# 28 of 76 projection groups by seven half-size products, with the weight scale worked out on GpSimd

## The chip, the cores and the metric

The kernel runs on one core of one Trainium2 chip. The metric is the device time of one execution in microseconds, the median over runs. The engines go by the names of the profile: PE is TensorE (matmul), PEld its weight loads, DVE is VectorE, ACT is ScalarE, POOL is GpSimd, and SP is SyncE, which issues most transfers. PSUM is the memory that TensorE writes to, SBUF the memory on the core that all engines read, and DRAM holds inputs, outputs and spilled data.

## The reference

Two layers run one after the other over 512 tokens of width 2048. Each layer projects the normalised input once, feeds three groups of heads, and projects their joined outputs back into the residual.

```
h    = x * rsqrt(mean(x*x) + EPS) * norm_g                # 512 x 2048
proj = h @ w_in                                           # 2048 x 8208, split by columns:
       # conv h,b,c,gate: 512 each; attention q,k,v,gate: 1024 each;
       # linear attention q,k: 256 each, v,gate: 512 each, low rank: 16
y_conv = cv_b * (conv3(cv_c * cv_h) + bias) * silu(cv_g)
q, k   = rmsnorm(sb_q), rmsnorm(sb_k)                     # 8 heads of 128
y_sb   = stick_breaking(q, k, v) * silu(sb_g)             # causal, 128 queries at a time
   # z = q.k; log_keep = log_sigmoid(-z); w = exp(log_sigmoid(z) + sum of later log_keep); out = w @ v
g      = log_sigmoid(gl_lr @ w_up + b_up) / 16
y_gla  = rmsnorm(gla(q, k, v, g)) * silu(gl_g)            # 4 heads, chunks of 64 with a state
x      = x + concat(y_conv, y_sb, y_gla) @ w_out          # 2048 x 2048
```

Everything is float32. Nearly all of the multiplications are in `h @ w_in` and `mix @ w_out`.

## The kernel before, in words

**Groups.** The columns of `w_in` (2048 x 8208) and `w_out` (2048 x 2048) are cut into groups of 256, one of them with the 16 low-rank columns on top. `specs` lists them in the order of their use: per layer 6 for the linear attention, 4 for the first half of the convolution, 16 for the attention (four times value, gate, query, key), 4 for the second half of the convolution, and 8 for the output, so 38 per layer and 76 in all.

**Two float16 parts.** TensorE multiplies float16. Every float32 operand is scaled by a power of two and split into a high part (rounded) and a low part (what the rounding left). A product is high x high + low x high + high x low, three matmuls for every one of the reference.

**A group's way.** `fetch` (called two groups ahead, transfers by SP) brings two halves of 1 MB, 128 partitions x 8 x 256, into `stage`. `wmax` (L319) squares each half on ScalarE and keeps the sums. `wscale` (from L329) adds them over partitions on GpSimd (`wgm`) and makes from the sum, on VectorE, the scale `ws` and its inverse `wu` in five or six instructions on single numbers (L330 to L348). `whi` (L392) writes the high parts on ScalarE, `wlo` (L399) the low parts on VectorE. `load` does all of it for group i+1 when group i is taken up, at high priority; the squares of a group are kept behind the last high part of the group before.

**Products.** `project_cols` (L568 to L570) keeps a block of weights stationary and moves all 512 tokens: 96 matmuls of 512 columns. `project_toks` (L576 to L578) keeps activations of 128 tokens stationary and moves the 256 columns of the group: 192 matmuls. `project_by_token` (L601) is the same, token block by token block. Results go to two PSUM banks of `psp`, which has three.

**The activations** are in `xh` and `xl`, and for the output in `mh` and `ml` (`mix`). Each of the 16 blocks of the joined branch outputs is split as soon as it is made, in `mixsplit`, each branch with a scale of its own (`mixscale`, column j of `pmix`); the weights of the output groups take the ratio of these scales into account block by block (`weight_ratio`, `wsr`).

**Attention.** `attend` puts four pieces of work into the list `later` (`scores` of two heads, `values` of two heads); `go` runs one of them between the projections of the next step. The gate of a branch (`gate`) is silu by exponent and logarithm.

**Output.** For each output group the old residual comes from DRAM into `qT`; `finish` (L1078) adds `psp` times `wu` to it on VectorE, stores the sum, and in the first layer squares it (L1084, ScalarE) for the next layer's norm.

**Order.** Each engine executes its instructions in the order in which the program was scheduled; a waiting instruction holds up those behind it on its engine. The start is written out by hand; elsewhere the order follows from the code, the priorities and the number of buffers in each pool (`stage` 3 halves, `wpool` 3 pairs of parts, `psp` 3 banks).

Of the kernel before, what the change touches and what calls it, by code (L numbers as in the profile page):

```python
# [20 lines left out]
XBITS = 8.0  # L21
RED = bass_isa.ReduceOp

# [7 lines left out]
CHUNKS = ((((3, 0), (2, 512)), (3, 2)), (((0, 0), (1, 128)), (0, 1)))  # L31


@with_exitstack
def hybrid_trunk(ctx, tc, x, norm_g, w_in, conv_w, conv_b, sb_qn_g, sb_kn_g,
# [10 lines left out]
    GX = GW + LR  # L46
    NG = D // GW
# [4 lines left out]
    big = ctx.enter_context(tc.tile_pool(name="big", bufs=4))  # L52
# [32 lines left out]
    xs = dram.tile([seq, D], F32, tag="xs", name="xs")  # L85
    xt = [newbig("x", [P, 2, D], F32) for _ in range(2)]
# [22 lines left out]
    parno = wk([P, 32], "raw", 1)  # L109
# [130 lines left out]

    V.tensor_scalar(xsc.bitcast(I32), xun.bitcast(I32), -1.0, float(254 << 23), ALU.mult, ALU.add)
# [30 lines left out]
    specs = []  # L272
    for l in range(depth):
        for cols in ([(GL_V, GW)], [(GL_V + GW, GW), (GL_LR, LR)], [(GL_Q, GW)], [(GL_K, GW)],
                     [(GL_G, GW)], [(GL_G + GW, GW)]):
            specs.append((l, w_in, cols))
        conv = [[(l, w_in, [(c0 + j * GW, GW)]) for c0 in (CV_H, CV_C, CV_G, CV_B)] for j in range(2)]
        specs += conv[0]
        for j in range(4):
            for c0 in (SB_V, SB_G, SB_Q, SB_K):  # L280
                specs.append((l, w_in, [(c0 + j * GW, GW)]))
        specs += conv[1]
        for gi in range(NG):
            specs.append((l, w_out, [(gi * GW, GW)]))
# [10 lines left out]
    def junk(n):  # L295

        return wk([P, HK * GX], "junk", 1, dt=U8)[:, :n]


    def fetch(i):  # L300

        l, src, cols = specs[i]
        staged[i] = st = []
        for h in range(2):
            s_ = stage.tile([P, HK, GX], F32, tag="st", name=nm("st"))
            o = 0
            for c0, w in cols:
                nc.sync.dma_start(
                    s_[:, :, o:o + w],
                    src[l, h * HK * P:(h + 1) * HK * P, c0:c0 + w].rearrange("(k p) n -> p k n", p=P))  # L310
                o += w
            st.append(s_)

    def wmax(i, h):

        n = sum(c[1] for c in specs[i][2])
        if h == 0:
            peak[i] = sm(2, "wm")
        S.activation(junk(HK * n).rearrange("p (k n) -> p k n", k=HK), staged[i][h][:, :, :n], AF.Square,  # L319
                     accum_out=peak[i][:, h:h + 1])  # L320

    def wscale(i):

        l, src, cols = specs[i]

        m = sm(1, "wq")
        if i:
            gm = sm(2, "wgm")
            G.partition_all_reduce(gm, peak.pop(i), P, RED.add)  # L329
            V.tensor_scalar(m, gm[:, 0:1], gm[:, 1:2], 2.0 ** -120, ALU.add, ALU.max)  # L330
        else:
# [5 lines left out]
            V.tensor_scalar(m, ps, 2.0 ** -120, None, ALU.max)  # L337
        V.tensor_scalar(m.bitcast(I32), m.bitcast(I32), 0x7F000000, None, ALU.bitwise_and)
        sc = sm(1, "ws")
        V.tensor_scalar(sc.bitcast(I32), m.bitcast(I32), -0.5, float(204 << 23), ALU.mult, ALU.add)  # L340
        p2 = sm(1, "wp")
        V.tensor_scalar(p2.bitcast(I32), m.bitcast(I32), 0.5, float(50 << 23), ALU.mult, ALU.add)
        u = sm(1, "wu", bufs=6)
        sw = None
        if src is w_out:
            sw = sm(8, "wsr")
            V.tensor_scalar(sw, ratio[l][0], sc, None, ALU.mult)
# [781 lines left out]
```

## Time and profile before

| What | Value | How to read it |
|---|---|---|
| time of the runs | 1742.44 us, median of 3 (1742.14 to 1742.74) | the metric |
| span of the profiled execution | 1740.9 us | first to last instruction of one execution |
| TensorE (PE) | 1726.8 us busy, 12,846 matmuls | idle 7.7 us of the first 40, 2.0 between 890 and 1020, 3.7 after 1560 |
| VectorE (DVE) | 1068.9 us busy, 2015 instructions | 282.3 us of it low parts of the `w_in` groups |
| ScalarE (ACT) | 1090.0 us busy, 1460 instructions | 285.5 us squares, 317.9 us high parts of weights |
| GpSimd (POOL) | 75.1 us busy, 104 instructions | 47.0 us of it sums over partitions for the weight scales |
| transfers | 204.69 MB, 118 GB/s on average | 1 MB halves of weights land 5.3 to 5.5 us after issue |

A row of the grouped view reads: line, engine, operation, output and inputs by the names in the program, their shapes, the count; then busy time in all, mean duration of one in ns; then the idle time of the engine just ahead of them and what ended it. A row of the timeline begins with start and duration. The first layer's output groups run up to about 890 us of the span, the second layer's from about 1560 us to the end.

### The profile page before, as it was taken

The numbers are of one execution on the slowest core, as the hardware profiler recorded it, in microseconds if no ns is written. First come the engines' busy times: TensorE is split into PE (matmuls) and PEld (weight loads), VectorE is DVE, ScalarE is ACT, GpSimd is POOL, SyncE is SP. The second block draws the span as 40 slices with busy tenths as digits, with TensorE's granted clock in tenths as the row PEclk, the third lists the DMA queues.
The fourth block names the chain that finished last, engine by engine and source line by source line (L and its number), as shares of the span: only waits on it lengthen the run. The fifth ranks groups of instructions, "written<-read, shape, count | busy, mean of one in ns | idle before, by whom it ended". The sixth has DMA issues, their size and how long they took to land.

```text
span 1740.9 us, 30651 instructions
## 1 busy us (share of the span) xinstructions
PE 1726.8 (99%) x12846; PEld 1232.4 (71%) x12846; DVE 1068.9 (61%) x2015; ACT 1090.0 (63%) x1460; POOL 75.1 (4%) x104
## 2 busy tenths in 40 slices
PE   8999999999999999999999999999999999999999
PEld 6744556868787754788885455668686868448888
DVE  7556788657665747433474576976575666673431
ACT  7558577667575867455555684766767667663540
POOL 1000000000000000000010000000000000000000
PEclk9999999999999999999999999999999999999999
DMA  6333313335353545444463333133454444453531
GB/s 222 121 97 97 98 58 113 103 104 131 108 140 110 128 121 128 134 158 146 138 148 105 97 97 97 50 121 110 125 124 109 117 124 126 112 132 113 177 124 40
DMA packets 266121, 204.69 MB, mean 118 GB/s; under 512 B 93106, under 2 KB 265212, under 8 KB 265472
## 3 DMA queue, kind: packets, MB, share of 16 engines
q1 hardware_dynamic: 256976, 193.29, 39.0%
q10 hardware_dynamic: 9008, 9.45, 1.6%
q8 instruction: 100, 1.64, 0.4%
q14 instruction: 37, 0.30, 0.1%
HBM read 173.36 MB, written 8.39 MB: 104 GB/s over the span
## 4 chain that ended last, share of the span: by engine, by line
PE 48%; issue 7%; DVE 1%; DMA 1%; SPq 0%; POOL 0%; ACT 0%; POOLq 0%; DVEq 0%
PE psp L576 8%; PE psp L578 8%; PE psp L577 8%; PE psp L570 6%; PE psp L568 6%; PE psp L569 6%; PE psp L601 3%; PE psz L749 1%; PE psm L988 1%; PE psz L944 1%; PE psz L840 0%; DMA m<-raw 0%; DVE wl L399 0%; SPq L487 0%; DMA xs<-x 0%
## 5 line engine op out<-in xcount | busy, mean ns | idle before, releaser
L577 PE MATMUL psp<-wl,m 128*128 128x256 f16 x1664 | 454.0, 273 | 0.0
L578 PE MATMUL psp<-wh,m 128*128 128x256 f16 x1664 | 453.9, 273 | 0.0
L576 PE MATMUL psp<-wh,m 128*128 128x256 f16 x1664 | 453.8, 273 | 0.0
L399 DVE SCALAR_TENSOR_TENSOR wl<-st,ws,wh 128x2048 f16<-128x2048 f32 (+1 forms) x120 | 282.3, 2353 | 193.1 <-ACT wh L392 179.7
L392 ACT ACTIVATE wh<-st,ws 128x2048 f16<-128x2048 f32 (+1 forms) x118 | 236.3, 2003 | 202.6 <-PE psp L569 100.9
L319 ACT ACTIVATE junk<-st 128x2048 uint8<-128x2048 f32 (+1 forms) x150 | 285.5, 1903 | 7.6 <-DMA st<-in_w_out_dram 4.5
L577 PE MATMUL psp<-wl,x 128*128 128x256 f16 x768 | 209.5, 273 | 0.0
L578 PE MATMUL psp<-wh,x 128*128 128x256 f16 x768 | 209.5, 273 | 0.0
L576 PE MATMUL psp<-wh,x 128*128 128x256 f16 x768 | 209.4, 273 | 0.0
L570 PE MATMUL psp<-m,wl 128*128 128x512 f16 x512 | 194.4, 380 | 0.0
L568 PE MATMUL psp<-x,wh 128*128 128x512 f16 x512 | 194.4, 380 | 0.0
L569 PE MATMUL psp<-x,wh 128*128 128x512 f16 x512 | 194.4, 380 | 0.0
L569 PE MATMUL psp<-m,wh 128*128 128x512 f16 x512 | 194.4, 380 | 0.0
L568 PE MATMUL psp<-m,wh 128*128 128x512 f16 x512 | 194.4, 380 | 0.0
L570 PE MATMUL psp<-x,wl 128*128 128x512 f16 x512 | 194.3, 380 | 0.0
L570 PEld LDWEIGHTS <-wl 128*128 128x128 f16 x1024 | 100.1, 98 | 122.8 <-issue 3.7
L569 PEld LDWEIGHTS <-wh 128*128 128x128 f16 x1024 | 100.1, 98 | 117.5 <-issue 1.1
L568 PEld LDWEIGHTS <-wh 128*128 128x128 f16 x1024 | 100.1, 98 | 115.3 <-issue 0.5
L576 PEld LDWEIGHTS <-m 128*128 128x128 f16 x1664 | 162.7, 98 | 19.9 <-issue 0.7
L578 PEld LDWEIGHTS <-m 128*128 128x128 f16 x1664 | 162.6, 98 | 19.4 <-issue 0.5
L577 PEld LDWEIGHTS <-m 128*128 128x128 f16 x1664 | 162.6, 98 | 18.8
L392 ACT ACTIVATE wh<-st,wsr 128x512 f16<-128x512 f32 x128 | 81.6, 710 | 100.5 <-PE psp L578 74.4
(285 smaller groups left out, 2260.4 us busy)
## 6 DMA issues: line engine op xcount, KB each, us to landing
st<-in_w_in_dram SPq DMA_DIRECT2D x120, 1024.0 KB, 5.3
st<-in_w_out_dram SPq DMA_DIRECT2D x32, 1024.0 KB, 5.5
x<-in_x_dram SPq DMA_DIRECT2D x4, 1024.0 KB
qT<-in_x_dram ACTq DMA_DIRECT2D x8, 512.0 KB, 5.3
qT<-xs ACTq DMA_DIRECT2D x8, 512.0 KB
xs<-x SPq DMA_DIRECT2D x14, 256.0 KB, 4.5
out_dram<-kT SPq DMA_DIRECT2D x14, 256.0 KB, 3.7
th<-za SPq DMA_TRANSPOSE x64, 3.6
```

The source lines that it names most:

```text
L319: S.activation(junk(HK * n).rearrange("p (k n) -> p k n", k=HK), staged[i][h][:, :, :n], AF.Square, accum_out=peak[i][:, h:h + 1])
L392: lasthi[i] = S.activation(wh[:, ks, :n], staged[i][h][:, ks, :n], AF.Copy, scale=s_)
L399: V.scalar_tensor_tensor(wl[:, ks, :n], staged[i][h][:, ks, :n], s_, wh[:, ks, :n], ALU.mult, ALU.subtract)
L568: T.matmul(o, wh[:, kk, cs], xh[:, :, k, :], start=st_, stop=False)
L569: T.matmul(o, wh[:, kk, cs], xl[:, :, k, :], start=False, stop=False)
L570: T.matmul(o, wl[:, kk, cs], xh[:, :, k, :], start=False, stop=en)
L576: T.matmul(o, ah[:, t, k, :], wh[:, kk, :n], start=st_, stop=False, skip_group_check=True)
L577: T.matmul(o, ah[:, t, k, :], wl[:, kk, :n], start=False, stop=False, skip_group_check=True)
L578: T.matmul(o, al[:, t, k, :], wh[:, kk, :n], start=False, stop=en, skip_group_check=True)
L601: T.matmul(o[:, :n], a_[:, t, k, :], w[k // HK][part][:, k % HK, :n], start=i == 0 and k == 0, stop=i == 2 and k == KT - 1)
L749: T.matmul(o, src16[sb][a][:, ss], tgt16[tb][b][:, g0:g1].rearrange("p g h c -> p (g h c)"), start=i == 0, stop=i == 2)
L944: T.matmul(z[:, o:o + (t + 1) * P], qT[:, a_, t, hh, :], kT[:, b_, :t + 1, hh, :], start=i == 0 and o % 512 == 0, stop=False, skip_group_c ...
```

## The change

**Seven products.** A group that the table `SEVEN` marks is computed as a 2 x 2 block product: the tokens in two halves of 256, the input width in two halves of 1024, and the columns in two halves of 128. Instead of eight block products there are seven, of sums and differences of blocks. Marked are, per layer, the gate and key groups of the four attention steps, the first group of the second half of the convolution, and output groups 2 to 6: 14 per layer, 28 in all. `cols7` has the weights stationary (gate and convolution groups), `toks7` the activations (key and output groups).

**Weights.** For a marked group `right` makes seven quarter parts (128 x 1024), with four sums or differences of the staged quarters on VectorE between them; `wpool` holds six quarter tiles with high and low part, `stage` four halves.

**Activations.** The sums of blocks are made once a layer for the input (`x_sums`, placed behind the low-rank gate: four operations on each of two tiles, eight splits, and transposing transfers by SP) and once a layer for the mix (`mix_sums`).

**Evictions.** `seven` leaves the results in four quarters, made from pieces in PSUM: `Raw` puts them together without scale, `Residual` with scale and the old residual.

**The scale.** `wscale` does its arithmetic on GpSimd behind the sum over partitions, in four instructions (`wq` twice, `ws`, `wu`); group 0 stays on VectorE. The power of two is taken by rounding the exponent with a large constant. Output groups use one scale for the whole mix, so the ratio is gone.

**The mix.** Branch outputs are spilled to DRAM unsplit (`spill` into `mixd`), loaded back into two tiles `m32` during the second half of the convolution (`mix_load`), and split there with the one scale of `mix_unit`.

**Values one step later.** The `values` of a step's second head are held until the next step, between its two `scores`.

**Shorter chains.** `gate` has three ScalarE operations on half a gate instead of five, `scores` two VectorE operations fewer on each chunk, and the sum over partitions of the value bound (`bgm`) is gone. Small products of scales (`nu`, `vu`, `qu2`, `uu`) are made on GpSimd.

```diff
-XBITS = 8.0
+XBITS = 7.0
+MAGIC = 12582912.0
+SEVEN = {"gla": (), "conv0": (), "sb": (1, 3), "conv1": (0,), "out": (2, 3, 4, 5, 6)}
...
-    stage = ctx.enter_context(tc.tile_pool(name="stage", bufs=3))
-    wpool = ctx.enter_context(tc.tile_pool(name="wpool", bufs=3))
+    stage = ctx.enter_context(tc.tile_pool(name="stage", bufs=4))
+    wpool = ctx.enter_context(tc.tile_pool(name="wpool", bufs=6))
...
     def wscale(i):
...
             G.partition_all_reduce(gm, pk, P, RED.add)
+            if pk.shape[-1] > 2:
+                G.tensor_tensor(gm[:, 0:1], gm[:, 0:1], gm[:, 2:3], ALU.add)
+            E = G
+            E.tensor_scalar(m, gm[:, 0:1], gm[:, 1:2], 2.0 ** -120, ALU.add, ALU.max)
...
+        E.tensor_scalar(m, m.bitcast(I32), 2.0 ** -24, MAGIC, ALU.mult, ALU.add)
         sc = sm(1, "ws")
+        E.tensor_scalar(sc.bitcast(I32), m, -(2.0 ** 23), (MAGIC + 204) * 2.0 ** 23, ALU.mult, ALU.add)
         u = sm(1, "wu", bufs=6)
+        E.tensor_scalar(u.bitcast(I32), m, 2.0 ** 23, ratio[l] if src is w_out else xub[:, l:l + 1],
+                        ALU.mult, ALU.add)
...
+    def right(i):
+        a, b = (staged[i][0][:, :, c * P:(c + 1) * P] for c in range(2))
+        c, d = (staged[i][1][:, :, c * P:(c + 1) * P] for c in range(2))
+        def part(x):
+            w = wtile(i)
+            hi, lo = (w[:, h, :HK * P].rearrange("p (k n) -> p k n", n=P) for h in range(2))
+            his.setdefault(i, []).append(S.activation(hi, x, AF.Copy, scale=scales[i]))
+            V.scalar_tensor_tensor(lo, x, scales[i], hi, ALU.mult, ALU.subtract)
+        part(a)
+        V.tensor_tensor(b, b, d, ALU.add)
+        V.tensor_tensor(a, a, b, ALU.add)
+        part(a)
+        part(c)
+        V.tensor_tensor(c, c, a, ALU.add)
+        V.tensor_tensor(a, a, d, ALU.subtract)
+        part(a)
+        part(b)
+        part(d)
+        part(c)
     def load_(i):
-        with tc.issue_after(lasthi[i - 1].ins):
+        with tc.issue_after(his[i - 1][min(1, len(his[i - 1]) - 1)].ins):
...
+    def seven(left, by_cols, evict):
...
+        o1 = bank(psp, "p")
+        product(o1, 0, True, False)
+        with tc.high_priority():
+            s1 = tmp("s1")
+            S.activation(s1, o1[:, :2 * P], AF.Copy, scale=ev.unit)
+        o2 = bank(psp, "p")
+        product(o2, 1, True, True)
+        with tc.high_priority():
+            u2 = tmp("u2")
+            ev.add(u2, o2[:, :2 * P], s1)
+        product(o1, 2, False, True)
+        ev.first(o1[:, :2 * P])
+        o3 = bank(psp, "p")
+        product(o3, 3, True, True)
...
+            ev.sub(vv, o3[:, :2 * P], u2)
+        o4 = bank(psp, "p")
+        product(o4, 4, True, False)
+        ev.last4(vv, o4[:, :2 * P])
+        product(o2, 5, True, True)
+        ev.plus(0, 1, o2[:, :2 * P], vv)
+        product(o4, 6, False, True)
+        ev.plus(1, 0, o4[:, :2 * P], u2)
...
+    def column_sums(pieces):
+        tt = V.tensor_tensor
+        for x11, x12, x21, x22 in pieces:
+            tt(x22, x21, x22, ALU.subtract)
+            tt(x21, x11, x21, ALU.subtract)
+            tt(x11, x22, x11, ALU.subtract)
+            tt(x12, x12, x11, ALU.add)
...
+        def mix_sums(s_):
...
+            for i, (th, kh) in ((1, (0, 0)), (0, (1, 1)), (2, (1, 0)), (3, (0, 1))):
...
+                for k in (0, HK // 2):
...
+                    S.activation(a, y, AF.Copy, scale=s_)
+                    V.scalar_tensor_tensor(b, y, s_, a, ALU.mult, ALU.subtract)
...
+            prior = held.pop() if held else lambda: None
+            if j < 3:
+                held.append(lambda: values(1))
+                later.extend((lambda: scores(0), prior, lambda: scores(1), lambda: values(0)))
...
+        y = conv_in(1, go)
+        m32 = mix_load()
+        s_ = conv_out(1, y, go)
...
+        for k in (0, 4, 6, 8, 12, 14, 10, 2):
+            mix_split(k, s_)
+        if any(modes[cursor[0]:cursor[0] + NG]):
+            sums = mix_sums(s_)
...
+            def last4(self, vv, ps):
...
+                V.tensor_tensor(r, self.like(vv), r, ALU.add)
+                with tc.high_priority():
+                    V.scalar_tensor_tensor(dst, self.like(ps), self.nu, r, ALU.mult, ALU.add)
```

**What moves.** In the rows below names carry buffer numbers; a row gives line, operation, output and inputs, and the shape.

GpSimd in the attention steps of the first layer, before: `wgm` is the sum over partitions of a group's squares, `bgm` that of the bound of the values.

```order
L169 ISA bgm_623_5169<-bm_578_4742 128x1
L329 ISA wgm_640_5240<-wm_636_5234 128x2
L329 ISA wgm_669_5516<-wm_665_5510 128x2
L329 ISA wgm_699_5800<-wm_695_5794 128x2
L329 ISA wgm_724_6082<-wm_720_6076 128x2
```

The same engine and stage with the change, where `wq`, `ws` and `wu` are the steps of the scale:

```order
L348 ISA
L348 ISA wgm_786_7166<-wm_782_7160 128x2
L352 ISA
L352 TENSOR_SCALAR wq_785_7165<-wgm_786_7166 128x1
L361 TENSOR_SCALAR wq_785_7165<-wq_785_7165 128x1
L363 TENSOR_SCALAR ws_787_7170<-wq_785_7165 128x1
L365 TENSOR_SCALAR wu_788_7172<-wq_785_7165,xub_155 128x1
L1257 TENSOR_SCALAR qu2_843_7871<-wu_788_7172 128x1
L348 ISA
L348 ISA wgm_823_7481<-wm_819_7475 128x2
```

Each sum over partitions now has an unnamed instruction ahead of it and another behind it, and four steps of arithmetic follow on the same engine.

ScalarE in the first layer's output groups, before: `junk, wm` are the squares of the next group's halves, `wh` its high parts, and L1084 the squares of the residual.

```order
L319 ACTIVATE junk_998_8571,wm_997_8570<-st_973_8316 128x2048
L319 ACTIVATE junk_999_8573,wm_997_8570<-st_974_8318 128x2048
L392 ACTIVATE wh_1006_8588<-st_973_8316,wsr_1005_8585 128x2x256 x4
L392 ACTIVATE wh_1008_8598<-st_974_8318,wsr_1005_8585 128x2x256 x4
L1084 ACTIVATE junk_1012_8804,ssq_903_7559<-x_901_7557 128x256
```

The same engine in the first marked output group with the change. `s1` is its first piece out of PSUM; the parts with scale `ws_992` are its own, those with `ws_1015` the next group's.

```order
L335 ACTIVATE junk_1011_9291,wm_1010_9290<-st_985_9033 128x2048
L680 ACTIVATE s1_1025_9378<-psp_1024_9329,wu_993_9049 128x256
L429 ACTIVATE w_997_9064<-st_964_8792,ws_992_9047 128x1024
L429 ACTIVATE w_998_9067<-st_964_8792,ws_992_9047 128x1024
L429 ACTIVATE w_999_9070<-st_965_8794,ws_992_9047 128x1024
L429 ACTIVATE w_1000_9073<-st_965_8794,ws_992_9047 128x1024
L335 ACTIVATE junk_1012_9293,wm_1010_9290<-st_986_9035 128x2048
L429 ACTIVATE w_1017_9304<-st_985_9033,ws_1015_9300 128x1024
L429 ACTIVATE w_1018_9309<-st_985_9033,ws_1015_9300 128x1024
L429 ACTIVATE w_1019_9312<-st_986_9035,ws_1015_9300 128x1024
```

The second square of the next group now stands behind the last part of this one, and the next group's first part directly behind that square.

VectorE at the same place with the change. `vv` and `x` are pieces of the output of the group with `wu_993`, `qT` its old residual.

```order
L1343 SCALAR_TENSOR_TENSOR vv_1029_9529<-psp_1028_9480,wu_993_9049,u2_1027_9429 128x256
L1354 TENSOR_TENSOR qT_1007_9284<-vv_1029_9529,qT_1007_9284 128x2x128
L1360 TENSOR_TENSOR qT_1007_9284<-vv_1029_9529,qT_1007_9284 128x2x128
L1356 SCALAR_TENSOR_TENSOR x_958_8783<-psp_1030_9531,nu_1031_9580,qT_1007_9284 128x2x128
L430 SCALAR_TENSOR_TENSOR w_1017_9304<-st_985_9033,ws_1015_9300,w_1017_9304 128x1024
L434 TENSOR_TENSOR st_985_9033<-st_985_9033 128x8x128
L1362 SCALAR_TENSOR_TENSOR x_957_8782<-psp_1026_9380,wu_993_9049,qT_1007_9284 128x2x128
L430 SCALAR_TENSOR_TENSOR w_1018_9309<-st_985_9033,ws_1015_9300,w_1018_9309 128x1024
L430 SCALAR_TENSOR_TENSOR w_1019_9312<-st_986_9035,ws_1015_9300,w_1019_9312 128x1024
L1362 SCALAR_TENSOR_TENSOR x_958_8783<-psp_1030_9531,wu_993_9049,qT_1007_9284 128x2x128
```

Before, both low parts of the next group stood ahead of a group's two output pieces; now the next group's first low part stands between the second and the third of four pieces, with one of its sums behind it, and two more low parts ahead of the last piece.

More of the change, by code (lines that the diff above doesn't have):

```diff
@@ L407, in load_ @@
         wscale(i)
-        for h in range(2):
-            whi(i, h)
-            wlo(i, h)
+        if modes[i]:
+            right(i)
+            return
+        for q in range(4):
+            whi(i, q)
+            wlo(i, q)
     def weights():
@@ L519, in hybrid_trunk @@
     xlow(0, 1, mix, True)
-    wlo(0, 0)
-    wlo(0, 1)
+    for q in range(4):
+        wlo(0, q)
     xhigh(1, 0, mix)
@@ new lines, in project_by_token, with quarters, own @@
+    def project_by_token(n):
+        w, u = weights()
+        for t in range(NT):
+            o = bank(psp, "p")
+            for i, (a_, part) in enumerate(((xh, 0), (xl, 0), (xh, 1))):
+                for k in range(KT):
+                    T.matmul(o[:, :n], a_[:, k, t, :], wview(w, part, k, n),
+                             start=i == 0 and k == 0, stop=i == 2 and k == KT - 1)
+            yield t, o, u
+    def quarters(sums):
+        def own(th, kh):
+            return [a[:, kh * HK:(kh + 1) * HK, 2 * th:2 * th + 2, :] for a in mix]
+        return own(0, 0), sums[1], own(0, 1), sums[0], sums[2], sums[3], own(1, 1)
```

575 lines of the change are left out of this document (357 added, 218 removed).

## The prediction

> **What bounds the kernel now.** I read the head of the page first, then who waited for whom on TensorE, then its timeline, then the stretches by stage, and last the groups by form on the engines that feed it.
>
> ```profile
> span 1740.9 us, 30651 instructions
> ...
> PE 1726.8 (99%) x12846; PEld 1232.4 (71%) x12846; DVE 1068.9 (61%) x2015; ACT 1090.0 (63%) x1460; POOL 75.1 (4%) x104
> ...
> PEclk9999999999999999999999999999999999999999
> ...
> PE 48%; issue 7%; DVE 1%; DMA 1%; SPq 0%; POOL 0%; ACT 0%; POOLq 0%; DVEq 0%
> ```
>
> TensorE is busy in 99% of the span at full granted clock, and the chain that ended last is its own work. A busy TensorE could still be a slow one, so its pace is read from the timeline, with start and duration in front.
>
> ```profile
> 30.26 1.91 PE L601 MATMUL psp<-wh,x 128*128 128x256 f16 x16
> 32.01 1.91 PE L601 MATMUL psp<-wl,x 128*128 128x256 f16 x16
> ...
> 157.98 1.50 PE L749 MATMUL psz<-m 128*128 128x128 f16 x24
> 159.32 0.38 PE L568 MATMUL psp<-x,wh 128*128 128x512 f16 x1
> 159.54 0.38 PE L569 MATMUL psp<-x,wh 128*128 128x512 f16 x1
> 159.75 0.38 PE L570 MATMUL psp<-x,wl 128*128 128x512 f16 x1
> ...
> 1716.33 20.97 PE psp L601 x192
> ```
>
> From start to start: 512 columns take 0.216 us, 256 columns 1.75/16 = 0.109, 128 columns 1.34/24 = 0.0558. A group of 192 matmuls of 256 columns takes 20.97 us, one of 96 matmuls of 512 takes 96 x 0.216 = 20.7. The engine runs at the pace of its columns, so fewer columns are time, if weights and activations keep coming.
>
> **The change part by part.** *Products.* 18 of the 28 groups have the activations stationary: 192 matmuls of 256 become 336 of 128, 336 x 0.0558 = 18.75 us, 2.22 less each, 40.0 in all. Ten have the weights stationary: 96 of 512 become 168 of 256, 168 x 0.109 = 18.4, 2.33 less each, 23.3 in all. Together -63.3 us. No matmul is added elsewhere; attention and the linear-attention part keep theirs. With the profiled execution's 1740.9 and the 1.5 us by which the median 1742.4 of the runs stands above it, the floor is 1679.
>
> *What feeds the products.*
>
> ```profile
> L399 DVE SCALAR_TENSOR_TENSOR wl<-st,ws,wh 128x2048 f16<-128x2048 f32 x116 | 272.4, 2349 | 186.7 <-ACT wh L392 173.2 <-PE psz L946 10.2 <-PE psz L749 2.9
> L1054 DVE SCALAR_TENSOR_TENSOR qp<-raw,qp 128x1024 f16<-128x1024 f32 x16 | 19.6, 1226 | 18.0 <-ACT qp L1053 18.0
> L902 DVE TENSOR_TENSOR kT<-kT,g 128x1024 f32<-128x1024 f32 x4 | 4.9, 1222 | 0.1
> L1078 DVE SCALAR_TENSOR_TENSOR kT<-psp,wu,qT 128x256 f32<-128x256 f32 x4 | 1.9, 484 | 18.8 <-PE psp L601 18.8
> L770 DVE TENSOR_TENSOR e<-raw 128x256 f32<-128x256 f32 x24 | 10.1, 422 | 3.1 <-PE psm L679 2.8
> L1053 ACT ACTIVATE qp<-raw 128x1024 f16<-128x1024 f32 x16 | 16.9, 1057 | 44.0 <-DVE raw L1049 25.8 <-DVE raw L1044 18.1
> L319 ACT ACTIVATE junk<-st 128x2048 uint8<-128x2048 f32 x146 | 277.4, 1900 | 7.5 <-DMA st<-in_w_out_dram 4.5 <-DMA st<-in_w_in_dram 1.2
> L319 ACT ACTIVATION_READ_ACCUMULATOR junk<-st 128x1 f32 x150 | 28.0, 187 | 0.0
> L1084 ACT ACTIVATE junk<-x 128x256 uint8<-128x256 f32 x32 | 13.3, 416 | 65.8 <-DVE x L1078 65.0 <-ACT junk L1084 0.3
> ```
>
> A plain group costs VectorE two low parts, 2 x 2.35 = 4.7 us. A seven-product group costs seven low parts of 1024 elements (7 x 1.23 = 8.6) and four adds (4 x 1.22 = 4.9), 13.5. Its output pieces, where they go into the residual, are six PSUM operations of 256 (6 x 0.48) and three adds (3 x 0.42), 4.2. That is 17.7 us for 18.75 us of TensorE: 94%.
>
> ```profile
> 340.00:640.00 300.00, 300.00 (x2401) 231.16 (x2399) 191.18 (x328) 205.99 (x247) 14.67 (x17) 1.00 0.47 121
> 705.00:890.00 185.00, 184.19 (x1665) 162.38 (x1663) 82.45 (x164) 99.02 (x172) 3.38 (x9) 1.00 0.51 151
> ```
>
> The columns are length, then busy time of PE, PEld, DVE, ACT, POOL, then clock and DMA. In the attention stage (first row) DVE is 64% and ACT 69% busy; eight of sixteen groups there get 8.8 more on DVE, less what the shorter score chain, gate and scale arithmetic give back. It stays under 80%. In the output stage (second row) DVE was 45% busy and goes beyond 90%, since the mix's splitting and sums (8 adds and 16 low parts of 1024, 29 us a layer) come on top. That cover is nearly gone; I allow 0.3 us for each of the 28 groups, 8 us, for output pieces that come late: each now has one product, 2.7 us, before TensorE wants the bank. The DRAM round trip costs nothing as long as its load hides behind the last three plain convolution groups, 62 us.
>
> *The scale on GpSimd.* Here a wait is added on the path that makes the weights.
>
> ```profile
> 740.52 0.19 ACT L319 ACTIVATION_READ_ACCUMULATOR junk<-st 128x1 f32 x1
> 742.26 2.56 ACT L392 ACTIVATE wh<-st,wsr 128x512 f16<-128x512 f32 x4 [1.55 <-DVE wu L348]
> ...
> 412.60 3.06 POOL L329 PARTITION_ALL_REDUCE wgm<-wm  x1 [21.40 <-ACT junk L319]
> ...
> 411.59 2.35 DVE L399 SCALAR_TENSOR_TENSOR wl<-st,ws,wh 128x2048 f16<-128x2048 f32 x1
> 413.85 1.56 DVE L965 TENSOR_TENSOR zw<-zw,za 128x895 f32<-128x895 f32 x2
> ...
> L169 POOLq MODIFY_POOL_CONFIG  x2: 11/11/11, 30.3 to 30.3; - x2
> ...
> 30.40 0.73 POOL L169 PARTITION_ALL_REDUCE kgm<-kg  x2
> ```
>
> From the last square to the first high part took 1.55 us. Two things lengthen that. First, an all-reduce of 0.4 us takes 3.06 where VectorE runs operations with two SBUF inputs back to back, and ends just behind them; GpSimd's steps (0.2 each, between VectorE's 0.15 and more) will meet that often. I take 2.0 us for reduce, three steps and such waits (1.0 to 4). Second, the order shows an unnamed GpSimd instruction ahead of every all-reduce and another ahead of the arithmetic; the kernel before has one, ahead of its first all-reduce, and there the trace has MODIFY_POOL_CONFIG. The change has 156. The one ahead of an all-reduce runs while it waits for the squares; the one behind it does not. Call its price t. The low end is the row: 0.1 us until the reduce starts. But the kernel before asks for one kind of code only, so no exchange need have taken place. If code has to come from DRAM, the nearest rows are landings:
>
> ```profile
> st<-in_w_in_dram SPq DMA_DIRECT2D x120, 1024.0 KB, 5.3
> ...
> st<-in_w_in_dram SPq DMA_DIRECT2D x4, 64.0 KB, 15.3
> ...
> ngr<-in_norm_g_dram ACTq DMA_DIRECT2D x1, 16.0 KB, 1.9
> ```
>
> 1.9 to 15.3 us; I take t = 5.3, the common landing, since an exchange is likelier than none. [...]
>
> Where t is hidden: in the attention stage long and short gaps between squares and first high part alternate on ACT (13 and 2 us of other work); ACT has some 30% idle there, eight short gaps of 5 us fit. Where it is not: in the first layer's output groups 2 to 6, where the first high part stands directly behind the squares. ACT's round there is seven high parts 7.4, two squares with their reads 4.2, four residual squares 4 x 0.6 = 2.4, one copy 0.4; the second high part waits for a low part and an add, 2.45; 0.6 for late output pieces; with the chain's 2.0 that makes 19.5 + t against 18.75. Behind the waiting high part stand VectorE's low part and, behind that, the last two output pieces, whose banks TensorE needs next, so the wait reaches it whole. Five handovers, less 3 us of head start at the first: 5 x (0.75 + 5.3) - 3 = 27 us. In the second layer the four remaining high parts (4.2) stand between, and the residual squares are gone: 17.6, hidden; I allow 2 for VectorE. At the start:
>
> ```profile
> 42.93 2.10 ACT L392 ACTIVATE wh<-st,ws 128x2176 f16<-128x2176 f32 x1
> ...
> 49.67 4.80 PE L601 MATMUL psp<-wh,x 128*128 128x272 f16 x40
> ```
>
> The second weight group's high part begins at 42.9 and TensorE takes it up at 49.7. Moved to 48.7, its four quarters (1.3 each) come about 4 us late.
>
> Sum: 1679 + 8 + 27 + 2 + 4 = **1720 us**.
>
> **The rivals.** *The exchange is free* (t = 0.1, the row of the trace). The output rounds are 19.6, 5 x 0.85 - 3 = 1; the start hides; 1679 + 8 + 1 + 2 = 1690. For it speaks the only row there is; against it, that this row never had to change the code.
>
> *The exchange is long, and the change loses.* The place is the same round. At t = 7.3 the parts are 37, 6 at the start, 7 in the second layer's rounds (20.2 against 18.75), and 12 in the attention stage and the hand-overs: 62, which eats the gain. Beyond that it is slower. At t = 9: 46 + 8 + 16 + 20 + 6 (the mix's scale waits for two exchanges before the output stage) = 96, 1775 us; GpSimd's own queue, 2t + 2.5 a group, then is 20.5 and sets the pace of the seven-product groups. For it speaks the 64 KB landing of 15.3 us; against it the common 5.3.
>
> *Matmuls of 128 columns don't keep 0.0558.* The row has 24 in a stretch; the change runs 336.
>
> ```profile
> L749 PEld LDWEIGHTS <-m x432: 97/98/98, 157.8 to 1152.0; 128*128 128x128 f16 x144
> ```
>
> Each matmul has its own weight load, recorded at 98 ns. If loads set the pace, the eighteen groups are worth nothing beyond 20.97/336 = 62 ns, and at 98 ns cost 18 x (32.9 - 18.75) = 255 more, 1975 us. Against it: in the 24 the loads overlap. [...]
>
> **How the numbers follow.** Forecast (t from 3 to 7.3) 0.35, 1706 to 1740; free exchange 0.27; long exchange 0.29; slow 128 columns 0.06; others 0.03. The range leaves out the slowest of the last three and a little below the free case: 1686 to 1800. A measurement of this kernel can tell some 0.2%, 3.5 us, from no change. Faster: 0.9 of the forecast and nearly all of the free case, 0.57. Slower: long exchange, slow columns and the rest, 0.36. Within: 0.07.
>
> **What would show it.** Right: about 18.8 us for a seven-product group in the attention stage, nothing waited for by TensorE there; in the first layer's output stage groups of about 25 us with ACT idle ahead of its first high part, put down to GpSimd's scale; GpSimd's gap between all-reduce and the first step near 5 us. Gaps of 0.1 and output groups under 20 us show the free case; gaps of 8 and more, with waits in the second layer and the attention stage too, the long one. Starts 70 ns and more apart within a product show slow columns. Waits of TensorE for output pieces in the attention stage, or for the mix's load, would make the prediction wrong in a way that none of the cases has.

## The result, and the profile after

The change makes the kernel slower: 1891.0 us in the median of four executions, three of them from 1888.2 to 1893.6, against 1742.6 before. The ratio is 1.085 (95% interval 1.083 to 1.086). One execution of the changed kernel and one each of two experiments' kernels took one and a half to over three times as long as the others of the same kernel and are left out of all ratios; without it the median of the changed kernel is 1888.4, so that differences from 1891.0 below are up to 2.6 us too large.

The head of the page of the changed kernel:

```profile
span 1891.9 us, 38254 instructions
...
PE 1728.7 (91%) x16158; PEld 1340.1 (71%) x16158; DVE 1310.1 (69%) x1972; ACT 1181.4 (62%) x1588; POOL 213.1 (11%) x452
...
PEclk8899999999999999988889999999999999998999
```

TensorE was idle for 14.1 us of the span before; now it is for 163.2. It is also as long at work as before, 1728.7 us, though the products should have taken 63.3 us off: the granted clock, 1.000 in the mean before, is 0.959, and below nine tenths in seven of the 40 slices. The view of who waited for whom shows where the idle time comes from (total in us, number of times, longest):

```profile
POOL wgm L348 <- ACT junk L335: 886.7, 70, 32.7
POOL wq L352 <- issue: 550.8, 73, 11.1
...
ACT w L429 <- POOL ws L363: 152.1, 22, 11.0
...
ACT w L412 <- POOL ws L363: 63.2, 12, 11.1
...
PE psp L669 <- ACT s L680: 28.2, 7, 5.1
...
PE psp L669 <- ACT w L429: 21.4, 6, 4.5
PE psz L1163 <- DMA kT<-qp: 21.1, 9, 4.9
```

Between each sum over partitions (`wgm`) and the first step of the scale (`wq`) GpSimd stands still for 7.5 us on average, waiting for nothing that the profile names. What stands there is in the list of the instructions of line 352 (duration in ns, first and last start):

```profile
L352 POOLq MODIFY_POOL_CONFIG  x146: 82/83/83, 65.2 to 1847.1; - x146
```

The instruction itself takes 0.083 us; the price comes behind it. ScalarE pays with 215 us of waits for `ws`, and TensorE's longest waits are for pieces and weights that ScalarE delivers late, and for transfers of the attention (`kT`).

### The profile page after: what moved, and what is told of

Read it like the earlier page. It is cut to its first block, busy times and chain, and to the rows that moved or that the text cites. A ratio compares the mean times of both kernels' runs of the same rounds, so it can differ in the third digit from the quotient of the medians.

```text
span 1891.9 us, 38254 instructions
## 1 busy us (share of the span) xinstructions
PE 1728.7 (91%) x16158; PEld 1340.1 (71%) x16158; DVE 1310.1 (69%) x1972; ACT 1181.4 (62%) x1588; POOL 213.1 (11%) x452
## 4 chain that ended last, share of the span: by engine, by line
PE 28%; ACT 22%; issue 22%; DVE 21%; DMA 3%; POOL 3%; ACTq 0%; POOLq 0%; SPq 0%; DVEq 0%
ACT junk L335 7%; ACT w L429 5%; PE psp L615 5%; PE psp L614 5%; PE psp L616 5%; PE psp L642 4%; DVE w L430 4%; ACT w L412 3%; PE psp L669 2%; PE psp L666 1%; POOL wgm L348 1%; DVE w L416 1%; DVE st L434 1%; DMA st<-in_w_out_dram 1%; DVE za L1178 1%
## 5 line engine op out<-in xcount | busy, mean ns | idle before, releaser
L430 DVE SCALAR_TENSOR_TENSOR w<-st,ws,w 128x1024 f16<-128x1024 f32 x196 | 246.8, 1281 | 197.9 <-ACT w L429 196.7
L429 ACT ACTIVATE w<-st,ws 128x1024 f16<-128x1024 f32 x196 | 217.9, 1141 | 242.9 <-POOL ws L363 152.1
L630 PE MATMUL psp<-w,act 128*128 128x256 f16 x1280 | 352.3, 275 | 14.2 <-ACT act L1068 11.7
L632 PE MATMUL psp<-w,act 128*128 128x256 f16 x1280 | 351.9, 275 | 2.2 <-DVE act L1069 2.2
L631 PE MATMUL psp<-w,act 128*128 128x256 f16 x1280 | 352.0, 275 | 0.0
L416 DVE SCALAR_TENSOR_TENSOR w<-st,ws,w 128x1024 f16<-128x1024 f32 x192 | 244.2, 1278 | 112.7 <-ACT w L412 112.1
L335 ACT ACTIVATE junk<-st 128x2048 uint8<-128x2048 f32 x150 | 284.7, 1898 | 6.8 <-DMA st<-in_w_in_dram 5.5
L412 ACT ACTIVATE w<-st,ws 128x1024 f16<-128x1024 f32 x188 | 212.1, 1141 | 123.0 <-POOL ws L363 63.2
L614 PE MATMUL psp<-act,w 128*128 128x512 f16 x704 | 267.1, 379 | 0.0
L615 PE MATMUL psp<-act,w 128*128 128x512 f16 x704 | 267.1, 379 | 0.0
L616 PE MATMUL psp<-act,w 128*128 128x512 f16 x704 | 267.0, 379 | 0.0
L669 PE MATMUL psp<-w,act 128*128 128x128 f16 x2592 | 174.8, 233 | 55.7 <-ACT s L680 28.2
L669 PEld LDWEIGHTS <-act 128*128 128x128 f16 x2592 | 167.9, 106 | 58.6 <-issue 58.2
L666 PEld LDWEIGHTS <-w 128*128 128x128 f16 x1680 | 165.8, 99 | 29.1 <-issue 7.4
L642 PE MATMUL psp<-w,act 128*128 128x256 f16 (+1 forms) x1152 | 144.7, 288 | 31.8 <-ACT w L412 11.5
L642 PEld LDWEIGHTS <-act 128*128 128x128 f16 x1152 | 117.1, 102 | 56.7 <-issue 16.2
L348 POOL PARTITION_ALL_REDUCE wgm<-wm x75 | 47.1, 628 | 944.4 <-ACT junk L335 886.7
L630 PEld LDWEIGHTS <-act 128*128 128x128 f16 x1280 | 126.4, 99 | 28.2 <-ACT act L1068 12.1
L631 PEld LDWEIGHTS <-act 128*128 128x128 f16 x1280 | 126.5, 99 | 19.9 <-issue 4.4
L632 PEld LDWEIGHTS <-act 128*128 128x128 f16 x1280 | 126.1, 99 | 19.9 <-DVE act L1069 4.5
L614 PEld LDWEIGHTS <-w 128*128 128x128 f16 x704 | 69.0, 98 | 82.1 <-issue 2.4
L616 PEld LDWEIGHTS <-w 128*128 128x128 f16 x704 | 68.9, 98 | 81.3 <-issue 0.9
```

The costliest lines, as they stand in the source:

```text
L335: S.activation(junk(HK * GW).rearrange("p (k n) -> p k n", k=HK), staged[i][h], AF.Square, accum_out=peak[i][:, h:h + 1])
L412: his.setdefault(i, []).append(S.activation(quarter(i, q, 0)[:, :, :GW], staged4(i, q), AF.Copy, scale=scales[i]))
L429: his.setdefault(i, []).append(S.activation(hi, x, AF.Copy, scale=scales[i]))
L430: V.scalar_tensor_tensor(lo, x, scales[i], hi, ALU.mult, ALU.subtract)
L614: T.matmul(o, wh, xh[:, k, :, :], start=st_, stop=False)
L615: T.matmul(o, wh, xl[:, k, :, :], start=False, stop=False)
```

## The experiments

Two theories at first. *Exchange*: the gap comes with GpSimd's change from a sum to arithmetic (an exchange of its code, I supposed; no trace shows code being loaded), and it, with what it makes late, is the whole loss. *Crowding*: VectorE has no room for the seven-product groups, and the gap fills time that would be lost anyway.

### All scale arithmetic on VectorE

```diff
-            E = G
+            E = V
-            G.tensor_scalar(nu, u, -1.0, None, ALU.mult)
+            V.tensor_scalar(nu, u, -1.0, None, ALU.mult)
...
```

(and so for `vu`, `qu2`, `uu` and the addition for the low-rank columns)

> The changed kernel with all scale arithmetic back on VectorE (the four steps of the weight scale and the small products nu, vu, qu2, uu); GpSimd keeps only sums over partitions and memsets. Exchange theory: the 7.5 us between each sum over partitions and the first step are an exchange of GpSimd's code, and they, with the lower clock that follows TensorE's gaps, are the whole loss. Then time 1680 to 1705 us, first-layer marked output groups 18.8 to 20 us instead of 28.4, mean clock 1.00, no gap on GpSimd behind its sums. Crowding theory: the marked groups are late because VectorE (adds, low parts, pieces) has no room, and GpSimd's gap only fills time that would be lost anyway. Then the marked output groups stay at 24 us or more, the clock at 0.97 or less, and the time above 1800 us.

Measured: 1708.3 us, ratio to the kernel before 0.980 (0.979 to 0.982), clock 0.996. The head of its page, and the row of its waits that takes the place of the 550.8 us:

```profile
span 1706.9 us, 37939 instructions
...
PE 1669.5 (98%) x16158; PEld 1304.4 (76%) x16158; DVE 1345.4 (79%) x2328; ACT 1185.8 (69%) x1588; POOL 66.1 (4%) x96
```

```profile
DVE wq L352 <- POOL wgm L348: 68.3, 38, 4.5
```

VectorE now waits 1.8 us for a sum, in 38 cases of 75, and in half of the 75 its first step starts 0.6 us or less behind the last square: the sum itself is not what is late on GpSimd. TensorE's idle time is 37.4 us, its work 57.3 us less than before, and it no longer waits for `kT`. The exchange theory holds: 182.7 us of the loss hang on where the scale and the small products made with it are worked out. (The time is 3 us above the theory's 1680 to 1705.) The marked output groups of the first layer take 19.6 us instead of 28.4. The stretches of the two kernels over those five groups (length, then busy time of PE, PEld, DVE, ACT, POOL, then clock), first of the change, then with all on VectorE:

```profile
809.90:952.20 142.30, 107.26 (x1681) 105.09 (x1681) 84.14 (x100) 68.58 (x101) 9.52 (x29) 0.87 0.38 123
```

```profile
748.10:846.20 98.10, 94.64 (x1683) 94.03 (x1681) 87.04 (x126) 70.87 (x106) 3.40 (x5) 1.00 0.55 179
```

The groups are timed by the first matmul of each, which gives the loss by place, as the sums of group lengths in us in the profiled executions:

| Groups | Before | Change | All on VectorE | Change less all on VectorE |
|---|---|---|---|---|
| first two, layer 1 | 54.6 | 71.6 | 65.6 | 6.0 |
| attention and two more, layers 1 and 2 | 824.2 | 866.5 | 785.4 | 81.1 |
| two ahead of the output, both layers | 89.4 | 111.2 | 93.2 | 18.0 |
| output, layer 1 | 167.7 | 218.6 | 162.1 | 56.5 |
| first two, layer 2 | 50.2 | 66.9 | 53.2 | 13.7 |
| output, layer 2 | 167.6 | 170.1 | 160.6 | 9.5 |

The remaining 16 groups, linear attention and first half of the convolution, are equal (365.2, 365.2 and 365.0).

### One step of four on GpSimd, in the change and in the kernel before

The first of these is the kernel with all on VectorE, the second the kernel before; in both the step that follows the sum over partitions is issued on GpSimd:

```diff
-            V.tensor_scalar(m, gm[:, 0:1], gm[:, 1:2], 2.0 ** -120, ALU.add, ALU.max)
+            G.tensor_scalar(m, gm[:, 0:1], gm[:, 1:2], 2.0 ** -120, ALU.add, ALU.max)
```

> As the kernel with all arithmetic on VectorE, but the first of the four steps of the weight scale stays on GpSimd. Exchange theory: the price is per change of code, not per step, so the gap of 7.5 us stays and the time is 1855 to 1895 us. Slow-steps theory (GpSimd's arithmetic is what is slow, three of four steps gone): the loss shrinks to about a quarter, 1730 us or less.

> The kernel before with one thing changed: the first step of the weight scale runs on GpSimd. Exchange theory: a gap of about 7.5 us on GpSimd behind each of 75 sums; most of it hides behind 21 us groups whose ScalarE has 9 us to spare, the rest shows at the start and at the layer boundary (8 us each) and as about 1 us in each first-layer output group: 1760 to 1790 us. If the gap in the changed kernel belongs to the seven products and not to the change of code: no gap here and 1742 to 1748 us.

Measured: 2157.3 and 2086.9 us, one execution each. The price per exchange is there, and it doesn't depend on the steps or on the seven products: from the sum to the step 6.7 us at least, 7.2 and 7.4 in the median, as in the change (6.7, 7.2). But both kernels are far slower than either theory said, and the first is slower than the change with all four steps on GpSimd. The waits of the one and of the other:

```profile
DVE wq L361 <- POOL wq L352: 580.8, 75, 12.0
```

```profile
DVE wq L338 <- POOL wq L330: 708.8, 75, 13.6
```

Now VectorE is the engine whose next instruction waits, 7.7 and 9.5 us in each of 75 groups, with everything it has to do queued behind: pieces of output, gates, scores. In the change only ScalarE's first high part waits, and often there is time for that. The first layer's eight groups of the linear attention and the convolution's first half (four of each, the first two left out) show it: 182.6 us before and in the change, 209.5 in the one kernel with a step on GpSimd and 227.3 in the other. I had priced the second kernel as if ScalarE waited.

### No group by seven products

```diff
-SEVEN = {"gla": (), "conv0": (), "sb": (1, 3), "conv1": (0,), "out": (2, 3, 4, 5, 6)}
+SEVEN = {"gla": (), "conv0": (), "sb": (), "conv1": (), "out": ()}
```

With all scale arithmetic on VectorE:

> The changed kernel with no group marked for seven products and all scale arithmetic on VectorE: what is left is the mix by way of DRAM, values one step later, shorter chains, quarter tiles. If these are neutral, as the prediction costed them: 1735 to 1750 us, all plain groups 20.7 to 22.8 us. If the mix's round trip or the new start holds TensorE up by itself: 1760 us or more, with the excess in the last groups before the output or in the first two.

With the scale on GpSimd, as in the change; this kernel was run twice, so that there are two texts, and the measured time is that of the second run:

> The change with no group by seven products, the scale on GpSimd; to be held against the same on VectorE (1763.1 us). If the exchange costs the same 183 us whatever the groups are: 1945 us. If it costs by what stands behind the waiting high part, plain groups with 9 of 21 us of weight work on ScalarE hide most of it outside of the start and the layer boundary: 1780 to 1830 us.

> The change with no group by seven products and the scale on GpSimd, as before under another label, where the granted clock was 0.625 through the whole of the one execution with TensorE busy for 99% of it: a disturbance that says nothing on the exchange. Undisturbed, by the place of the wait: 1780 to 1830 us; by a price that does not depend on the groups: 1945 us.

Measured: 1763.1 on VectorE (one execution), 1798.6 on GpSimd (ratio to the kernel before 1.033, 1.031 to 1.035). So the exchange costs 35.5 us where all groups are plain, and 182.7 with the seven products. In the plain kernel the gap is the same, as the view of waits has it:

```profile
POOL wq L352 <- issue: 533.6, 73, 9.4
```

but the attention stage does not feel it (845.7 us in both layers without the exchange, 842.7 with it): 30.3 of the 35.5 us are in the first two groups of each layer. Each theory had half of it: the gap is the cause, and the crowded round of the seven products decides what it costs.

The 1763.1 us say also that the rest of the change is not neutral, as I had costed it. In four gate groups TensorE stands still for 2.7 us ahead of `values`, each of which now runs one step later; these groups are 5.7 us longer than before. With the gate by seven products the same place shows no such wait. So the seven products are worth 54.8 us where the rest of the change is in place, near the 55 of the prediction (63.3 less 8), but the change without exchange is worth only 34.

### Small products on GpSimd, the scale on VectorE

The change with `E = V` for the weight scale; `nu`, `vu`, `qu2` and `uu` stay on GpSimd.

> The weight scale on VectorE, but the small products nu, vu, qu2 and uu on GpSimd as in the change: about 50 changes of code and back, none of them between a sum and the scale made from it. Place theory (the price of a change of code is paid only by who waits behind it): 1705 to 1735 us. Price theory (each change costs some microseconds of the whole wherever it stands): about 50/75 of the change's loss of 183 us, 1800 us or more.

Measured: 1725.7 us, one execution. Some 50 exchanges, there and back, cost 17.4 us: the place theory holds. 8 us of it are in the two groups ahead of each output stage, 7.5 in the output stages and none in the attention stages. The gap behind a sum is the same here, 7.2 us in the median.

### The scale on VectorE for output groups alone

```diff
-            E = G
+            E = V if src is w_out else G
```

> The change as it is, but the four steps of the weight scale run on VectorE for the 16 output groups and on GpSimd for the rest. If the loss belongs to the places where the wait stands, place by place: the eight output groups of the first layer took 218.6 us in the change and 162.2 with all on VectorE, those of the second 170.2 and 162.7; 1891 less 56 and 7 gives 1828 us, 1815 to 1840. If the attention stage takes over what the output stage gives back (GpSimd's queue as the bound): 1870 us or more.

Measured: 1819.5 us, ratio 1.045 (1.043 to 1.047). The output stages go back to 168.0 and 160.8 us, and the attention stages keep their loss (865.6 against 866.5): the loss is made place by place.

### The input's sums later

The kernel with all on VectorE leaves 29 us above the 1679 of the sum. The largest piece is at the start. VectorE there, with two rows of TensorE, in the kernel with all on VectorE:

```profile
45.37 0.16 DVE L350 TENSOR_TENSOR wgm<-wgm 128x1 f32<-128x1 f32 x1 [0.32 <-POOL wgm L348]
...
45.57 1.21 DVE L756 TENSOR_TENSOR x<-x 128x1024 f32<-128x1024 f32 x1
46.71 1.22 DVE L771 TENSOR_TENSOR qT<-x,qT 128x1024 f16<-128x1024 f32 x1
...
47.84 0.20 DVE L352 TENSOR_SCALAR wq<-wgm 128x1 f32<-128x1 f32 x1
47.96 1.21 DVE L753 TENSOR_TENSOR x<-x 128x1024 f32<-128x1024 f32 x1
49.10 1.22 DVE L771 TENSOR_TENSOR th<-x,th 128x1024 f16<-128x1024 f32 x1
...
50.23 0.14 DVE L361 TENSOR_SCALAR wq<-wq 128x1 f32<-128x1 int32 x1
...
50.63 1.21 DVE L754 TENSOR_TENSOR x<-x,x 128x1024 f32<-128x1024 f32 x1
51.76 1.22 DVE L771 TENSOR_TENSOR g<-x,g 128x1024 f16<-128x1024 f32 x1
52.89 0.14 DVE L363 TENSOR_SCALAR ws<-wq 128x1 int32<-128x1 f32 x1
...
53.08 2.34 DVE L511 TENSOR_TENSOR act<-psz,act 128x1024 f16<-128x1024 f32 x2
...
54.35 7.84 PE L642 MATMUL psp<-w,act 128*128 128x256 f16 x50 [4.96 <-DVE act L511]
```

Lines 753 to 756 and 771 are `x_sums`. In the code it stands behind the low-rank gate; the scheduler has pulled it into the start, where its 1.2 us operations stand between the steps of the second group's scale (8 us for four steps of 0.2) and ahead of the last input tile (L511), for which TensorE waits. The experiment holds the sums back behind the third group's last low part, first in both layers, then in the first alone:

```diff
+            los[i] = V.scalar_tensor_tensor(lo[:, :, :GW], ...)
...
         def x_sums():
+          with tc.issue_after(los[cursor[0]].ins):                                    # first
+          with tc.issue_after(los[cursor[0] if cursor[0] < 38 else 38].ins):          # second
             column_sums(...)
```

> All scale arithmetic on VectorE as in the first experiment (1708.3 us), and the input's sums of blocks are held back on VectorE behind the third weight group's last low part. Early-sums theory: the scheduler has pulled the eight sums and their low parts into the start and into the layer boundary, where they stand ahead of the tiles and of the second group's scale; the first group's 42.2 us (31.6 in the kernel before) and the second layer's 30.7 (27.7) go back, and the time is 1693 to 1699 us. Start-by-other-means theory (four instead of two parts, more instructions for the scale, one transfer more for the low-rank columns make the start late): the start stays and the time is 1705 to 1712 us.

> All scale arithmetic on VectorE; the input's sums are held back behind the third weight group in the first layer alone, where holding them gained 4.7 us in the group times; in the second layer, where it lost 6.5, they stay where they were: 1702 to 1706 us. If the places exchange their loss in full whatever is done: 1708 us.

Measured: 1708.5 us (ratio 0.981, 0.979 to 0.982) and 1704.6 (ratio 0.979, 0.977 to 0.980). The early-sums theory is right on the start, whose first two groups go from 65.6 to 54.7 us, and wrong on the time: in the eight groups behind, 6.3 us are lost in the first layer and 8.3 in the second, since the sums now stand between the steps of a later group's scale (10.6 us from the first to the third) and ahead of a piece for which TensorE waits 3.6 us. Held back in the first layer alone, they gain 3.8 us, as expected; this is the fastest kernel found.

### More and fewer groups by seven products

With all on VectorE; the first with the sums held back in both layers and the eight query groups marked as well, the second with no output group marked.

```diff
-SEVEN = {..., "sb": (1, 3), ..., "out": (2, 3, 4, 5, 6)}
+SEVEN = {..., "sb": (1, 2, 3), ..., "out": (2, 3, 4, 5, 6)}      # first
+SEVEN = {..., "sb": (1, 3), ..., "out": ()}                      # second
```

> As the kernel with the input's sums held back, and the query groups of the attention steps are computed by seven products too, eight groups more. If the pace of 0.0558 us for 128 columns is the only limit: 8 x 2.2 = 17.8 us less than that kernel. If VectorE's room in the attention stage is the limit (13.5 us of weight work in three of four groups): no gain or a loss against it.

> All scale arithmetic on VectorE, and the ten output groups are plain, so that the mix's sums of blocks are gone too. Ten groups by 2.2 us say 22 us more than the 1708.3 of the kernel with them: 1730 us. If VectorE's 94% in that stage and the mix's sums take a good part of it, as the group lengths (105.0 to 98.1 and 96.6) with 6 us in the groups ahead of them say: 1715 to 1720 us.

Measured: 1706.7 us (ratio 0.980, 0.978 to 0.982), no clear difference from the 1708.5 without the eight, and 1721.7 (ratio 0.988, 0.986 to 0.990). The attention stage of the first layer, without and with the query groups:

```profile
261.10:653.80 392.70, 390.81 (x4173) 344.22 (x4172) 321.78 (x551) 294.54 (x393) 8.43 (x18) 1.00 0.48 134
```

```profile
263.00:654.50 391.50, 383.89 (x4749) 344.48 (x4748) 358.11 (x598) 304.61 (x406) 14.13 (x18) 1.00 0.48 134
```

TensorE's work falls by 6.9 us and the stage by 1.2, while VectorE goes from 82% to 91% of it: this is what crowding says, though no run takes work off VectorE to show it. The ten output groups are worth 13.4 us of their 22.2.

## Why the prediction was wrong, step by step

The forecast of 1720 us lies 171 us below the measured 1891, and the changed kernel is slower; the range ended at 1800. By the steps:

- *Products, -63.3 us: right.* With all scale arithmetic on VectorE TensorE's work is 57.3 us less at a clock of 0.996, and the last marked output group takes 18.8 us, as worked out. Matmuls of 128 columns keep 0.0558 us through 336: the rival of slow columns is out.
- *VectorE's cover, 8 us: right in size.* With all scale arithmetic on VectorE the marked output groups are 7.1 us above their pure pace in both layers together, and the output group ahead of them is 2.5 us longer; this group is back at 20.96 in the kernel without marked output groups, which makes no sums of the mix. The two groups ahead of the output stage are as long there, 93.2 us, so their 3.8 us are not the sums'. VectorE is busy for 82% of the first layer's attention stage, where the prediction had under 80.
- *The price of the exchange, t = 5.3: the mis-sized term.* It was taken from the common landing of a transfer; measured are 6.7 to 11.1 us, 7.2 in the median, and 9.0 in the first layer's marked output groups; why it is longer there stays open. The traces show the instruction, 0.083 us long, and the gap behind it, but not what fills the gap.
- *The round in the first layer's output groups, 19.5 + t: right.* With 9.0 it gives 28.5; measured are 28.4. ScalarE's wait stands where the prediction put it. The rows of one handover in the changed kernel, on GpSimd, ScalarE, VectorE and TensorE:

```profile
883.89 0.85 POOL L348 PARTITION_ALL_REDUCE wgm<-wm  x1 [17.07 <-ACT junk L335]
...
893.79 0.31 POOL L352 TENSOR_SCALAR wq<-wgm 128x1 f32<-128x1 f32 x1 [9.05 <-issue]
...
894.69 1.15 ACT L429 ACTIVATE w<-st,ws 128x1024 f16<-128x1024 f32 x1 [10.94 <-POOL ws L363]
...
895.88 1.28 DVE L430 SCALAR_TENSOR_TENSOR w<-st,ws,w 128x1024 f16<-128x1024 f32 x1 [9.29 <-ACT w L429]
...
895.89 0.26 PE L669 MATMUL psp<-w,act 128*128 128x128 f16 x1 [4.53 <-ACT w L429]
```

- *"ACT has some 30% idle there, eight short gaps of 5 us fit": the step that failed.* The attention stages lose 81 us by the exchange, where I had put nothing, and no more than a share of 12 (at t = 7.3) in the rival of the long exchange. The small products on GpSimd cost nothing there when the scale is on VectorE, so the 81 are the scale's. The prediction had named waits of TensorE for output pieces in the attention stage as a sign that none of its cases covers; six of the seven waits for `s` are there, 26.6 us. ScalarE at the weights of one key group in the change, and then at the same place with all on VectorE; the TensorE rows at 409.47 and 396.77 begin the query group that runs meanwhile:

```profile
409.24 0.19 ACT L335 ACTIVATION_READ_ACCUMULATOR junk<-st 128x1 f32 x1
...
409.47 0.27 PE L630 MATMUL psp<-w,act 128*128 128x256 f16 x1
...
417.87 1.15 ACT L429 ACTIVATE w<-st,ws 128x1024 f16<-128x1024 f32 x1 [6.55 <-POOL ws L363]
...
436.56 3.23 ACT L429 ACTIVATE w<-st,ws 128x1024 f16<-128x1024 f32 x3 [3.75 <-DVE st L438]
...
444.18 0.39 ACT L680 ACTIVATE s<-psp 128x256 f32<-128x256 f32 x1
...
444.62 3.62 PE L669 MATMUL psp<-w,act 128*128 128x128 f16 x36 [4.20 <-ACT s L680]
```

```profile
396.55 0.19 ACT L335 ACTIVATION_READ_ACCUMULATOR junk<-st 128x1 f32 x1
...
396.77 0.27 PE L630 MATMUL psp<-w,act 128*128 128x256 f16 x1
...
399.22 1.14 ACT L429 ACTIVATE w<-st,ws 128x1024 f16<-128x1024 f32 x1
...
426.10 0.39 ACT L680 ACTIVATE s<-psp 128x256 f32<-128x256 f32 x1
```

  Counted from the start of the query group, the first high part begins after 8.4 us in the one and 2.5 in the other, and the eviction `s` of the key group's first product after 34.7 and 29.3. So the high part is 5.9 us late and the eviction still 5.4, although ScalarE is idle for 5.8 us between the two. Most of that idle time is the wait at 436.56 for a sum on VectorE (`st`), which itself stands behind a low part made from the late weights: it can't be used to catch up. With all on VectorE the eviction ends 1.1 us before TensorE wants the bank again, so 4.2 us of the delay reach TensorE.
- *The start, 4 us: wrong, with a cause I did not have.* It is 17 us late: 11 by the input's sums, which I had read from the code and not from the order of VectorE, and 6 by the exchange.
- *The layer boundary and the groups ahead of the output* lose 13.7 and 18.0 us by the exchange, 8 of the 18.0 by that of the small products. The rival of the long exchange named both places, with 6 us for the second and 20 for the first and the attention stage together at t = 9.
- *The second layer's output rounds, hidden but for 2 us: too small.* (The 17.6 leaves out the 0.6 for late pieces that the first layer's round has.) The five marked groups take 20.3 us each on average instead of 18.75; the rival had 20.2 for t = 7.3. Of these 7.9 us, 2.7 are there with all on VectorE, and 5.2 go with the exchange.
- *What follows a gap of TensorE: not in the sum at all.* In the changed kernel TensorE's busy time is 59.2 us above that with all on VectorE, for the same matmuls. The row at 444.62 shows it: 36 matmuls in 3.62 us, 0.1 us each behind a wait of 4.2. Just ahead of that wait 48 of them took 2.84 us:

```profile
437.58 2.84 PE L669 MATMUL psp<-w,s 128*128 128x128 f16 x48
```

  In the first layer's output groups the granted clock is 0.87, as the stretch above has it. Behind the changed kernel's waits of 3.1 us and more, starts of matmuls of 128 columns are 107 ns apart instead of 56 (in the row at 444.62 from the tenth on), and behind none of the eight waits of 1.4 to 1.6 after the first 20 us. This lasted for 27 to 54 matmuls of 128 columns, 2.9 to 5.8 us, and three waits of 2.3 to 2.4 us were followed by it too.

The rival of the long exchange was the right one. It was put at break-even for t = 7.3 (its parts with the 8 us of cover give 1749) and at 1775 for 9 (1783 with that cover, which the sum leaves out), because most of the attention stage and the lower clock were missing from it: at the measured 7.5 the exchange costs 183 us, where the rival's parts for 7.3 came to 62. The order had shown the 156 instructions; the sum took the exchange where ScalarE waited with nothing else to do, and gave it away elsewhere.

## What to carry to other kernels

An engine that changes between two kinds of work can pay some microseconds at each change, on GpSimd here 6.7 to 11.1, that no row of the kernel before shows; count the changes in the order of instructions, and look for work that lets the engine stay with one kind. What such a wait costs is decided by the engine whose next instruction stands behind it: 35 us with slack on ScalarE, 183 us in a crowded round, 449 us when VectorE itself waited. And hiding is to be shown by following the order from the late instruction to the one that TensorE needs, not by an engine's share of idle time.

## What the runs showed of the hardware

- Between a sum over partitions and arithmetic on single numbers on GpSimd the trace of the change has MODIFY_POOL_CONFIG (146 records, two for each of 73 steps), and from the sum to the first step it took 6.7 to 11.1 us, 7.2 in the median. With one step instead of four it took as long: 6.7 us at least, 7.2 in the median.
- In the changed kernel, after its first 20 us, every wait of TensorE of 2.3 us and more was followed by matmuls at half pace (107 ns from start to start instead of 56 for 128 columns), and none of the eight of 1.4 to 1.6; for the same 16,158 matmuls the busy time was 1669.5, 1728.7 and 1777.0 us in kernels in which TensorE was idle for 37, 163 and 379 us.
